# Where a minus sign is applied and who adds two small sums in the set-up of a state-space layer

## The chip, the cores and the metric

One core of a Trainium2 chip. The metric is device time in microseconds (us) for one launch of the whole program, as the median of several runs; lower is better. The engines are named as the profile names them: PE (TensorE matmul) and PEld (its weight loads), DVE (VectorE), ACT (ScalarE), POOL (GpSimd), SP (SyncE, which here only issues DMAs).

## What is computed

One encoder layer on 3 x 1024 tokens of width 1024: RMSNorm, one input projection, two parallel branches, an output projection, a residual and a final RMSNorm. Branch A is a gated MLP that mixes positions within chunks of 128. Branch B, which the change touches, is a diagonal complex state-space layer (S5): 64 groups of 16 channels, 64 complex states per group, one scan forward and one backward, a skip term D and a GELU.

```python
bb_re = fr[..., None] * b_re - fi[..., None] * b_im      # the input matrices B
bb_im = fr[..., None] * b_im + fi[..., None] * b_re
# scan: s[t] = a * s[t-1] + B x[t]     (complex, per state)
y = einsum('ntgp,gcp->ntgc', sr, c_re) - einsum('ntgp,gcp->ntgc', si, c_im)
y = (y_fwd + y_bwd) + d_skip * xb                        # D skip
```

Only the real part of C times the state is wanted, so the imaginary part of the state enters with a minus.

## The kernel before

**Blocks of 8 steps.** The S5 scan is done over blocks of 8 positions. For each group the kernel builds, once, an input matrix (8 x 16 inputs to the states), an output matrix with a real and an imaginary half (states to 8 x 16 outputs, powers of a times C), and a small kernel of 16 x 16 matrices for what happens within one block, whose diagonal matrix of lag 0 also carries D. They go to DRAM (`mat_d`, `ks_d`) and are read back in the second stage.

**First stage** (`p1`, up to about 372 us in the profiled execution). The main work on PE is the projection to the S5 input: 48 blocks of 24 matmuls of 128x512 (`sweep`, `mm3`, lines 59 to 61). Beside it run the norm of the token halves (`norm_half`, lines 253 to 292) and, one piece per matmul block, the generator `s5_setup`. Its first pieces make the powers and B and C; its last 32 pieces are the loop at lines 1026 to 1032: `build(gp)` makes the matrices for two groups, then `finish` completes those of the pair before.

**`build`** (lines 953 to 998). The real half `pc` number 0 is made by DVE: two products (967, 968) and their difference (970). The imaginary half, number 1, has its two products on POOL (967, 968), but its sum is made on DVE (972), as minus the first product minus the second, which puts the minus of the reference into the matrix. The products' buffers `m1`, `m2` of each half are single, so POOL's next products (989, 990, for the input matrix `pb`) wait until line 972 has read them. Line 991 adds them, on DVE for half 0 and on POOL for half 1. Line 997 copies B into zero-padded tiles `Bm`, four copies of 64x32 on POOL. The DMAs at line 975 (four per step) are issued by ACT.

**`finish`** (lines 1000 to 1023). Eight matmuls (1007) multiply `Bm` with `pc` into one PSUM tile `s5b`, of which there is one buffer. Two ACT copies (1010, 1011) bring it to SBUF as `ksb`; DVE adds the lag-0 part of the other direction straight from PSUM (1012); two DVE instructions (1015), one per group, add the identity scaled by D. Then a DMA, four PE transposes of `pb` into `s5a` (1020), an ACT copy and a DMA.

**Second stage.** `s5_groups` runs 64 groups beside the other projections; `states` (1107 to 1137) rotates, scans and rotates back the states: products at 1131 and 1132, then a difference for the real half (1133) and a sum for the imaginary half (1134).

A planner orders each engine's instructions when the program is built, by priority and the order of the code; at run time each engine works through its own list in that order and waits on semaphores. POOL also makes the low halves of the split weights (`whl`, line 152), which every matmul block needs.

Of the kernel before, what the change touches and what calls it, by code (L numbers as in the profile page):

```python
# [11 lines left out]
F32 = mybir.dt.float32  # L12
# [4 lines left out]
ALU = mybir.AluOpType  # L17
# [11 lines left out]
CH = 16  # L29
# [10 lines left out]
def bcast(ap, shape):  # L40
    return ap.to_broadcast(shape)
# [15 lines left out]
def mm3(nc, out, lh, ll, rh, rl, first, last):  # L57

    nc.tensor.matmul(out, lh, rh, start=first, stop=False)  # L59
    nc.tensor.matmul(out, lh, rl, start=False, stop=False)  # L60
    nc.tensor.matmul(out, ll, rh, start=False, stop=last)  # L61
# [699 lines left out]
def s5_setup(st, tc, a, xpool, ps, ident, kio, f8h, f8l, r8, ks_d, mat_d):  # L761
# [3 lines left out]
    V, S, G, T = nc.vector, nc.scalar, nc.gpsimd, nc.tensor  # L765
# [8 lines left out]
    dcol = mpool.tile([CH, GRP], F32, name="dcol")  # L774

    with ExitStack() as tmp_st:
# [7 lines left out]
        def tt(x, y, op, out=None):  # L784
            o = out if out is not None else new(x.shape)
            V.tensor_tensor(o, x, y, op=op)
            return o
# [82 lines left out]
        m2 = tt(mag, mag, ALU.mult)  # L870
# [44 lines left out]
        for t, n in ((Cr, "c_re"), (Ci, "c_im")):  # L915
            for q in range(2):
                craws = []
                for i in range(4):
                    raw = tp.tile([P, 2, 64], F32, name="craw", tag="craw", bufs=4)
                    g0 = 8 * (4 * q + i)  # L920
# [26 lines left out]
    wp = st.enter_context(tc.tile_pool(name="wp", bufs=2))  # L947
# [5 lines left out]
    def build(gp):  # L953
        g0 = 2 * gp
        gs = slice(g0, g0 + 2)

        sh = [P, 2, 9, CH]
        cr = bcast(Cr[:, gs].unsqueeze(2), sh)
        ci = bcast(Ci[:, gs].unsqueeze(2), sh)
        ar, ai = (bcast(t[:, :, gs].rearrange("p n g -> p g n").unsqueeze(3), sh) for t in AO)  # L960
        pcl = []
        for i, (u, v) in enumerate(((ar, ai), (ai, ar))):
            e = V if i == 0 else G
            m1 = wp.tile(sh, F32, tag=f"m1{i}", name="m1", bufs=1)
            m2 = wp.tile(sh, F32, tag=f"m2{i}", name="m2", bufs=1)
            pc = wp.tile(sh, F32, tag=f"pc{i}", name="pc")
            e.tensor_tensor(m1, cr, u, op=ALU.mult)
            e.tensor_tensor(m2, ci, v, op=ALU.mult)
            if i == 0:
                V.tensor_tensor(pc, m1, m2, op=ALU.subtract)  # L970
            else:
                V.scalar_tensor_tensor(pc, m1, -1.0, m2, op0=ALU.mult, op1=ALU.subtract)
            for d in range(2):
                r = slice(64 * d, 64 * d + 64)
                dma(mat_d[gs, r, 256 + P * i:384 + P * i].rearrange("g p (j c) -> p g (j c)", j=J),
                    pc[r, :, 1 - d:9 - d].rearrange("p g j c -> p g (j c)"))
            pcl.append(pc)

        sh = [P, 2, J, CH]
        br = bcast(Br[:, gs].unsqueeze(2), sh)  # L980
        bi = bcast(Bi[:, gs].unsqueeze(2), sh)
        ar, ai = (bcast(t[:, :, gs].rearrange("p n g -> p g n").unsqueeze(3), sh) for t in AI)
        pbs = []
        for i, (u, v) in enumerate(((ar, ai), (ai, ar))):
            m1 = wp.tile(sh, F32, tag=f"m1{i}", name="m1", bufs=1)
            m2 = wp.tile(sh, F32, tag=f"m2{i}", name="m2", bufs=1)
            pb = wp.tile(sh, F32, tag=f"pb{i}", name="pb")
            e = V if i == 0 else G
            e.tensor_tensor(m1, br, u, op=ALU.mult)
            e.tensor_tensor(m2, bi, v, op=ALU.mult)  # L990
            e.tensor_tensor(pb, m1, m2, op=ALU.subtract if i == 0 else ALU.add)
            pbs.append(pb)
        bm = Bm[gp % 2]
        for i, bt in enumerate((Br, Bi)):
            for d in range(2):
                r = slice(64 * d, 64 * d + 64)
                G.tensor_copy(bm[r, i, :, 32 * d:32 * d + 16], bt[r, gs])
        return gp, pcl, pbs, bm

    def finish(gp, pcl, pbs, bm):  # L1000
        g0 = 2 * gp
        gs = slice(g0, g0 + 2)

        pk = ps.tile([48, 2, 144], F32, tag="s5b", name="s5b")
        for g in range(2):
            for i in range(2):
                T.matmul(pk[:, g], bm[:, i, g], pcl[i][:, g].rearrange("p j c -> p (j c)"),
                         start=i == 0, stop=i == 1)
        ksb = wp.tile([CH, 2, 240], F32, tag="ksb", name="ksb", bufs=1)
        S.copy(ksb[:, :, 0:128], pk[32:48, :, 16:144])  # L1010
        S.copy(ksb[:, :, 128:240], pk[0:16, :, 16:128])
        V.tensor_tensor(ksb[:, :, 112:128], ksb[:, :, 112:128], pk[0:16, :, 0:16], op=ALU.add)
        for g in range(2):
            o = ksb[:, g, 112:128]
            V.scalar_tensor_tensor(o, ident[0:CH, 0:CH], dcol[:, g0 + g:g0 + g + 1], o, op0=ALU.mult, op1=ALU.add)
        dma(ks_d[gs].rearrange("g c o -> c g o"), ksb)
        pp = ps.tile([P, 2, 2, P], F32, tag="s5a", name="s5a")
        for i in range(2):
            for g in range(2):
                T.transpose(pp[:, g, i], pbs[i][:, g].rearrange("p j c -> p (j c)"), ident)  # L1020
        pbt = wp.tile([P, 2, 256], F32, tag="pbt", name="pbt", bufs=1)
        S.copy(pbt.rearrange("p g x -> p (g x)"), pp.rearrange("p g i x -> p (g i x)"))
        dma(mat_d[gs, :, 0:256].rearrange("g p x -> p g x"), pbt)

    last = None
    for gp in range(GRP // 2):
        cur = build(gp)
        if last:
            finish(*last)
        last = cur  # L1030
        yield
    finish(*last)


def s5_groups(tc, sp, ps, small, kio, f8h, f8l, r8, xb_d, ks_d, mat_d, gy_d):
# [3 lines left out]
    V, S, G, T = nc.vector, nc.scalar, nc.gpsimd, nc.tensor  # L1039
# [5 lines left out]
    gp = sp.tile([P, 2 * KK + 2], F32, name="gt")  # L1045
# [61 lines left out]
    def states(g):  # L1107
        u, mi = st[g]
        tb = st.pop(("tab", g))
        cs = tb[:, 0:1].to_broadcast(sh)  # L1110
        sn = tb[:, 1:2].to_broadcast(sh)

        pb = ps.tile([P, 2, 512], F32, tag="pb", name="pb")[:, :, 0:KK]
        for i in range(2):
            mm3(nc, pb[:, i], mi[:, 0, i], mi[:, 1, i], u[:, 0], u[:, 1], True, True)
        b1 = sp.tile(sh, F32, tag="b1", name="b1")
        b2 = sp.tile(sh, F32, tag="b2", name="b2")
        V.tensor_tensor(b1, pb, cs, op=ALU.mult)  # L1118
        V.tensor_tensor(b2, pb[:, ::-1], sn, op=ALU.mult)
        V.tensor_tensor(b1[:, 0], b1[:, 0], b2[:, 0], op=ALU.add)  # L1120
        V.tensor_tensor(b1[:, 1], b1[:, 1], b2[:, 1], op=ALU.subtract)
        dec = st.pop(("dec", g))
        bf = b1.rearrange("p i k -> p (i k)")
        for r, o, z in ((slice(0, 64), gp[:, 2:2 * KK + 2], (0, P)), (slice(64, 128), gp[:, 0:2 * KK], (P - 1, KK - 1))):
            f = slice(None, None, 1 if r.start == 0 else -1)
            V.tensor_tensor_scan(o[r, f], dec[r, f], bf[r, f], 0.0, op0=ALU.mult, op1=ALU.add)  # L1126
            V.memset(gt[r, :, z[0]:z[1] + 1:z[1] - z[0]], 0.0)
        h = sp.tile([P, 2] + sh[1:], F32R, tag="h", name="h", bufs=2)
        h1 = sp.tile(sh, F32, tag="b1", name="h1")
        h2 = sp.tile(sh, F32, tag="b2", name="h2")  # L1130
        V.tensor_tensor(h1, gt, cs, op=ALU.mult)  # L1131
        V.tensor_tensor(h2, gt[:, ::-1], sn, op=ALU.mult)  # L1132
        V.tensor_tensor(h1[:, 0], h1[:, 0], h2[:, 0], op=ALU.subtract)
        V.tensor_tensor(h1[:, 1], h1[:, 1], h2[:, 1], op=ALU.add)
        V.tensor_copy(h[:, 0], h1)
        V.tensor_tensor(h[:, 1], h1, h[:, 0].bitcast(F32), op=ALU.subtract)
        st[g] = u, h
# [33 lines left out]
    for g in range(GRP):  # L1171
        states(g)
        store()
        if g < GRP - 1:
            prepare(g + 1)
        if g % 2 == 0 and g < GRP - 2:
            tables(g + 2)
        if g % 2 == 1 and g < GRP - 1:
            finish_tables(g + 1)
        yield  # L1180
        if g:
            outputs(g - 1)
        if g < GRP - 1:
            prepare_out(g + 1)
            decay(g + 1)
        if g < GRP - 2:
            issue(g + 2)
        if g == GRP - 1:
            store()
            outputs(g)  # L1190
            store()
        yield
# [30 lines left out]
```

## Time and profile before

| | us |
|---|---|
| median of 3 runs | 2521.51 (2518.17 to 2525.8) |
| the profiled execution | 2519.67 |
| its span, first to last instruction | 2517.7 |
| PE busy | 2439.0 (97%) |
| DVE busy | 1771.5 (70%) |
| ACT busy | 974.3 (39%) |
| POOL busy | 638.2 (25%) |
| granted TensorE clock, mean | 0.990 of full |

How to read it: a busy share is a mean over stages with different limits. POOL is busy for a quarter of the whole, but nearly all of its work lies in the first stage. What a change to the first stage is worth is therefore read from windows of that stage, from the waits within it, and from the order of a few instructions.

### The profile page before, as it was taken

How to read it: one execution, taken by the hardware profiler on the slowest of the kernel's cores; microseconds unless marked ns; L12 is line 12 of the kernel's file. 1: busy time of each engine (PE TensorE's matmuls, PEld its weight loads, DVE VectorE, ACT ScalarE, POOL GpSimd, SP SyncE). 2: the span in 40 equal slices, each digit the busy share in tenths (PEclk: the TensorE clock that was granted, in tenths of full speed). 3: DMA queues.
4: the chain of work that ended last, by engine and by line, in shares of the span. 5: the costliest groups of instructions: out<-in, count | busy, mean ns of one | idle time of the engine just before them, and what ended most of it. 6: DMA issues, size and time to landing. Idle time of an engine off the chain costs nothing.

```text
span 2517.7 us, 34046 instructions
## 1 busy us (share of the span) xinstructions
PE 2439.0 (97%) x12313; PEld 2077.4 (83%) x12313; DVE 1771.5 (70%) x2921; ACT 974.3 (39%) x1738; POOL 638.2 (25%) x623
## 2 busy tenths in 40 slices
PE   7999999989999899999999999999999999999998
PEld 5777779978888798888899888887888888888886
DVE  6888856899999879988898989755555533333332
ACT  5343334544554534544454443424343411111110
POOL 2579873345334302311130321101000100000000
PEclk9999999999999999999999999999999999999999
DMA  9565455355555534444453444456465732222220
GB/s 243 178 187 145 143 162 183 118 173 176 184 169 198 170 110 129 143 160 144 139 171 119 127 136 149 135 168 181 134 184 158 234 109 93 92 96 94 96 76 30
DMA packets 363017, 367.21 MB, mean 146 GB/s; under 512 B 40768, under 2 KB 308576, under 8 KB 350560
## 3 DMA queue, kind: packets, MB, share of 16 engines
q1 hardware_dynamic: 311008, 343.99, 43.1%
q10 hardware_dynamic: 51840, 21.04, 3.5%
q8 instruction: 97, 1.59, 0.3%
q14 instruction: 72, 0.59, 0.1%
HBM read 229.76 MB, written 135.20 MB: 145 GB/s over the span
## 4 chain that ended last, share of the span: by engine, by line
PE 70%; DVE 15%; DMA 2%; issue 1%; POOL 1%; ACT 1%; SPq 0%; ACTq 0%; DVEq 0%; POOLq 0%
PE mm L59 18%; PE mm L61 18%; PE mm L60 18%; PE acc L59 3%; PE acc L60 3%; PE acc L61 3%; DVE gt L1126 3%; PE py L59 1%; PE py L61 1%; PE py L60 1%; DVE h L1132 1%; DVE v L578 1%; DVE h L1131 1%; DVE b L1118 1%; DVE v L479 1%
## 5 line engine op out<-in xcount | busy, mean ns | idle before, releaser
L59 PE MATMUL mm<-w,yh 128*128 128x512 f32 x768 | 302.6, 394 | 0.0
L60 PE MATMUL mm<-w,yh 128*128 128x512 f32 x768 | 301.8, 393 | 0.0
L61 PE MATMUL mm<-w,yh 128*128 128x512 f32 x768 | 301.3, 392 | 0.0
L59 PE MATMUL mm<-ha,whl 128*128 128x512 f32 x704 | 278.3, 396 | 8.4 <-DVE v L503 7.4
L59 PE MATMUL mm<-hb,whl 128*128 128x512 f32 x704 | 278.0, 395 | 6.0 <-DVE v L503 6.0
L61 PE MATMUL mm<-ha,whl 128*128 128x512 f32 x704 | 275.9, 392 | 1.3 <-POOL whl L152 1.3
L60 PE MATMUL mm<-ha,whl 128*128 128x512 f32 x704 | 275.9, 392 | 0.0
L60 PE MATMUL mm<-hb,whl 128*128 128x512 f32 x704 | 275.8, 392 | 0.0
L61 PE MATMUL mm<-hb,whl 128*128 128x512 f32 x704 | 275.6, 392 | 0.0
L1126 DVE TENSOR_TENSOR_SCAN gt<-dec,b 64x768 f32<-64x768 f32 x128 | 232.2, 1814 | 3.1
L152 POOL TENSOR_TENSOR whl<-wf,whl 128x512 fp32r<-128x512 f32 x112 | 171.9, 1549 | 231.4 <-ACT whl L151 198.5
L61 PEld LDWEIGHTS mm<-w,yh 128*128 128x128 f32 x768 | 144.3, 188 | 33.7
L59 PEld LDWEIGHTS mm<-w,yh 128*128 128x128 f32 x768 | 144.1, 188 | 33.2
L60 PEld LDWEIGHTS mm<-w,yh 128*128 128x128 f32 x768 | 144.2, 188 | 33.0
L700 DVE SCALAR_TENSOR_TENSOR yh<-yf,yh 128x512 fp32r<-128x512 f32 x96 | 66.8, 699 | 147.6 <-ACT yh L699 106.0
L1057 POOL TENSOR_TENSOR mo<-m,mo 128x384 fp32r<-128x384 f32 x64 | 86.5, 1351 | 321.2 <-ACT mo L1056 321.2
L729 DVE TENSOR_TENSOR xr<-xr,mm 128x512 f32<-128x512 f32 x48 | 33.0, 688 | 184.1 <-PE mm L61 184.1
L59 PEld LDWEIGHTS mm<-ha,whl 128*128 128x128 f32 x704 | 133.1, 189 | 35.3 <-DVE v L503 8.3
L59 PEld LDWEIGHTS mm<-hb,whl 128*128 128x128 f32 x704 | 133.3, 189 | 32.1 <-DVE v L503 7.0
L61 PEld LDWEIGHTS mm<-ha,whl 128*128 128x128 f32 x704 | 133.0, 189 | 29.6 <-POOL whl L152 1.7
L61 PEld LDWEIGHTS mm<-hb,whl 128*128 128x128 f32 x704 | 133.2, 189 | 28.0
L60 PEld LDWEIGHTS mm<-ha,whl 128*128 128x128 f32 x704 | 133.2, 189 | 26.6 <-DVE ha L288 0.9
(243 smaller groups left out, 5946.1 us busy)
## 6 DMA issues: line engine op xcount, KB each, us to landing
whl<-wc_d SPq DMA_DIRECT2D x64, 1024.0 KB
wc_d<-whl SPq DMA_DIRECT2D x32, 1024.0 KB
wf<-in_w_in_dram SPq DMA_DIRECT2D x112, 256.0 KB
m<-mat_d SPq DMA_DIRECT2D x128, 128.0 KB
xb_d<-xo SPq DMA_DIRECT2D x24, 512.0 KB
U<-xb_d SPq DMA_DIRECT2D x64, 192.0 KB
gy_d<-gy SPq DMA_DIRECT2D x64, 192.0 KB
zb_d<-zb SPq DMA_DIRECT2D x24, 512.0 KB
```

Source lines behind the costliest of these rows:

```text
L59: nc.tensor.matmul(out, lh, rh, start=first, stop=False)
L60: nc.tensor.matmul(out, lh, rl, start=False, stop=False)
L61: nc.tensor.matmul(out, ll, rh, start=False, stop=last)
L152: G.tensor_tensor(flat[:, 1, sl], wf, flat[:, 0, sl].bitcast(F32), op=ALU.subtract)
L479: V.tensor_scalar(v, v, rs[:, q:q + 1], nb[:, q:q + 1], op0=ALU.mult, op1=ALU.add)
L578: V.scalar_tensor_tensor(t, t, LG[:, fb:fb + 1], RB[:, fb:fb + 1].to_broadcast([P, 4, P]), op0=ALU.mult, op1=ALU.add)
L700: V.scalar_tensor_tensor(y[:, 1], yf, sc, y[:, 0].bitcast(F32), op0=ALU.mult, op1=ALU.subtract)
L729: V.tensor_tensor(x, x, t.ps[i], op=ALU.add)
L1057: eng.tensor_tensor(t[:, 1], src, t[:, 0].bitcast(F32), op=ALU.subtract)
L1118: V.tensor_tensor(b1, pb, cs, op=ALU.mult)
L1126: V.tensor_tensor_scan(o[r, f], dec[r, f], bf[r, f], 0.0, op0=ALU.mult, op1=ALU.add)
L1131: V.tensor_tensor(h1, gt, cs, op=ALU.mult)
```

## The change

The minus of the imaginary output half is taken out of the matrix and put into the two things it is multiplied with. The sum at line 972 becomes a plain sum on the engine that made its products, POOL. The imaginary B is written into `Bm` times -1 (POOL, `tensor_scalar` for `tensor_copy`), and in the second stage the imaginary state is written as minus the one term minus the other (DVE, `scalar_tensor_tensor` for `tensor_tensor`). Apart from that, POOL makes in `build` a tile `dg` of 16 x 2 x 16 with D on the diagonals, and `finish` adds it to the PSUM part (`l0`) and that to `ksb`: two DVE additions in place of one addition and two scaled ones.

```diff
             e.tensor_tensor(m1, cr, u, op=ALU.mult)
             e.tensor_tensor(m2, ci, v, op=ALU.mult)
-            if i == 0:
-                V.tensor_tensor(pc, m1, m2, op=ALU.subtract)
-            else:
-                V.scalar_tensor_tensor(pc, m1, -1.0, m2, op0=ALU.mult, op1=ALU.subtract)
+            e.tensor_tensor(pc, m1, m2, op=ALU.subtract if i == 0 else ALU.add)
...
-                G.tensor_copy(bm[r, i, :, 32 * d:32 * d + 16], bt[r, gs])
-        return gp, pcl, pbs, bm
-
-    def finish(gp, pcl, pbs, bm):
+                if i == 0:
+                    G.tensor_copy(bm[r, i, :, 32 * d:32 * d + 16], bt[r, gs])
+                else:
+                    G.tensor_scalar(bm[r, i, :, 32 * d:32 * d + 16], bt[r, gs], -1.0, None, op0=ALU.mult)
+
+        dg = wp.tile([CH, 2, CH], F32, tag="dg", name="dg")
+        G.tensor_tensor(dg, ident[0:CH, 0:CH].unsqueeze(1).to_broadcast([CH, 2, CH]),
+                        dcol[:, gs].unsqueeze(2).to_broadcast([CH, 2, CH]), op=ALU.mult)
+        return gp, pcl, pbs, bm, dg
+
+    def finish(gp, pcl, pbs, bm, dg):
...
-        V.tensor_tensor(ksb[:, :, 112:128], ksb[:, :, 112:128], pk[0:16, :, 0:16], op=ALU.add)
-        for g in range(2):
-            o = ksb[:, g, 112:128]
-            V.scalar_tensor_tensor(o, ident[0:CH, 0:CH], dcol[:, g0 + g:g0 + g + 1], o, op0=ALU.mult, op1=ALU.add)
+        l0 = wp.tile([CH, 2, CH], F32, tag="l0", name="l0", bufs=1)
+        V.tensor_tensor(l0, dg, pk[0:16, :, 0:16], op=ALU.add)
+        V.tensor_tensor(ksb[:, :, 112:128], ksb[:, :, 112:128], l0, op=ALU.add)
...
-        V.tensor_tensor(h1[:, 1], h1[:, 1], h2[:, 1], op=ALU.add)
+        V.scalar_tensor_tensor(h1[:, 1], h1[:, 1], -1.0, h2[:, 1], op0=ALU.mult, op1=ALU.subtract)
```

## Rows read from the trace of the kernel before

**Rows 1.** Busy time by stretch: us, then each engine's (x count), PEclk, DMA share, GB/s.
```profile
core 0: us, PE busy (x) PEld busy (x) DVE busy (x) ACT busy (x) POOL busy (x), PEclk, DMA share, GB/s
94.00:207.00 113.00, 103.27 (x510) 82.12 (x508) 96.75 (x195) 44.48 (x90) 92.32 (x130) 0.95 0.62 187
...
303.00:358.00 55.00, 53.54 (x272) 42.38 (x271) 35.76 (x78) 16.61 (x36) 51.43 (x74) 1.00 0.55 155
...
600.00:1640.00 1040.00, 1022.12 (x5522) 906.04 (x5521) 925.63 (x1293) 485.53 (x837) 259.01 (x191) 0.99 0.47 150
```

**Rows 2.** PE's waits, 90 to 372 us: total us, times, longest us.
```profile
PE s5b L1007 <- DVE ksb L1012: 7.8, 7, 1.4
PE tr L283 <- DVE x L275: 4.0, 5, 2.3
PE s5b L1007 <- DVE rxa L51: 2.6, 1, 2.6
```

**Rows 3.** PE's instructions in order: start us, duration us, [idle before it, releaser].
```profile
319.70 0.54 PE L1007 MATMUL s5b<-pc,Bm 128*48 128x144 f32 x3 [1.44 <-DVE ksb L1012]
...
341.28 1.15 PE L1007 MATMUL s5b<-pc,Bm 128*48 128x144 f32 x8
342.36 0.66 PE L1020 MATMUL s5a<-ident,pb 128*128 128x128 f32 x4
```

**Rows 4.** DVE's instructions in order, ahead of the wait at 319.70.
```profile
317.23 1.53 DVE L972 SCALAR_TENSOR_TENSOR pc<-m,m 128x288 f32<-128x288 f32 x1 [3.42 <-POOL m L968]
318.69 0.42 DVE L989 TENSOR_TENSOR m<-Br,AI 128x256 f32<-128x256 f32 x1
...
319.38 0.17 DVE L1012 TENSOR_TENSOR ksb<-ksb,s5b 16x32 f32<-16x32 f32 x1
```

**Rows 5.** POOL's instructions in order, two stretches.
```profile
317.16 1.29 POOL L152 TENSOR_TENSOR whl<-wf,whl 128x512 fp32r<-128x512 f32 x1
...
338.02 0.73 POOL L991 TENSOR_TENSOR pb<-m,m 128x256 f32<-128x256 f32 x1
338.83 0.71 POOL L967 TENSOR_TENSOR m<-Cr,AO 128x288 f32<-128x288 f32 x1
339.49 0.71 POOL L968 TENSOR_TENSOR m<-Ci,AO 128x288 f32<-128x288 f32 x1
```

**Rows 6.** POOL's waits, 90 to 372 us: total us, times, longest us.
```profile
POOL m L989 <- DVE pc L972: 16.4, 8, 6.0
...
POOL whl L152 <- ACT whl L151: 6.4, 4, 3.3
POOL m L989 <- DVE rxy L53: 2.1, 1, 2.1
```

**Rows 7.** Groups of POOL, then of DVE, 90 to 372 us: busy us, mean ns | idle before.
```profile
L997 POOL COPY Bm<-Bi 64x32 f32<-64x32 f32 x64 | 26.7, 417 | 3.2
L968 POOL TENSOR_TENSOR m<-Ci,AO 128x288 f32<-128x288 f32 x32 | 26.2, 818 | 0.0
...
L972 DVE SCALAR_TENSOR_TENSOR pc<-m,m 128x288 f32<-128x288 f32 x32 | 25.3, 790 | 28.1 <-POOL m L968 20.5 <-DMA mat_d<-pc 3.4 <-DMA x<-in_x_sample_dram 2.1
```

**Rows 8.** Single lines of the whole execution: duration ns min/median/max, first and last start.
```profile
L972 DVE SCALAR_TENSOR_TENSOR pc<-m,m x32: 439/459/1551, 99.3 to 354.6; 128x288 f32<-128x288 f32 x32
...
L970 DVE TENSOR_TENSOR pc<-m,m x32: 439/760/1374, 97.8 to 349.8; 128x288 f32<-128x288 f32 x32
...
L1012 DVE TENSOR_TENSOR ksb<-ksb,s5b x32: 167/169/177, 117.6 to 366.8; 16x32 f32<-16x32 f32 x32
...
L1015 DVE SCALAR_TENSOR_TENSOR ksb<-ident,dcol,ksb x64: 215/217/699, 118.1 to 367.1; 16x16 f32<-16x16 f32 x64
...
L997 POOL COPY Bm<-Br x64: 202/329/675, 98.4 to 354.8; 64x32 f32<-64x32 f32 x64
```

**Rows 9.** DVE's instructions in order, second stage.
```profile
665.28 0.55 DVE L1134 TENSOR_TENSOR h<-h,h 128x384 f32<-128x384 f32 x1
665.75 0.60 DVE L1067 SCALAR_TENSOR_TENSOR tab<-kio,f8h,tab 128x384 f32<-128x384 f32 x1
```

## The prediction

> **What bounds the kernel now.** I read the busy time by stretch first [rows 1]. PE is busy over 97% of the span, so any gain must come out of PE's gaps. The stretch where nearly all of the changed code runs, 94 to 358 us, is different from the rest: POOL, a quarter busy over the whole, is at 92.3 of 113 us at its beginning and at 51.4 of 55 at its end, while DVE falls from 96.8 of 113 to 35.8 of 55. The reader is to see that the engine which gets work is the fuller one, the one which gives it the emptier one, at least late in the stage.
>
> Second, what PE waits for there [rows 2]: 7.8 us in seven waits of the product s5b for the DVE addition at line 1012 (s5b has one buffer, so the next product waits until line 1012 has read it), 4.0 us for normalised rows, 2.6 us for a DVE chain of the norm. That is what this change can win on PE directly.
>
> Third, why line 1012 is late [rows 3 to 5]. At 317.16 POOL starts a weight split of 1.29 us. At 317.23 DVE starts line 972, for whose products it had been idle 3.42 us; it needs 0.44 us when it runs alone [rows 8] but takes 1.53, until 0.3 us after POOL's split has ended at 318.45. Lines 989 and 990 follow, then line 1012 at 319.38, and PE starts at 319.70, 0.15 us after its end and after 1.44 us of waiting. DVE is not slow: it waits for POOL's products, then for POOL's split.
>
> **What holds two engines apart.** Line 1012, with one operand in PSUM, takes 167 to 177 ns all 32 times; line 1015, with both tensors in SBUF, 215 to 699; the two sums at lines 970 and 972 from 439 up to 1374 and 1551 [rows 8]. POOL's products go from about 0.66 us (one start to the next at 338.83 and 339.49 [rows 5]) to a mean of 0.82 [rows 7]. DVE instructions with two SBUF inputs and POOL's take turns.
> The Trainium skill (SBUF — State Buffer, "Who interferes with whom") says so: a DVE instruction with two SBUF inputs contends with a GpSimd instruction that reads SBUF, and whichever starts second is blocked for the whole of the other. The rows agree (1.53 us against 0.44). It speaks against the change as well as for it, since the sum moved to POOL occupies the shared read longer than it did on DVE.
>
> **Part by part.**
> *Sum of the imaginary half to POOL, 32 times.* DVE loses 25.3 us (32 x 0.79) and the 28.1 us of idle time ahead of it [rows 7], none of which counts by itself, as DVE is not PE's limit but through line 1012. POOL gets a 128x288 sum: at least 0.66 us (the product's spacing), 0.82 (its mean) at most; since it reads what was just written, as line 991 does (0.73 us and 0.81 to the next start for 256 columns), I take 0.80: 25.6 us. Behind it on POOL stand the weight splits and the next products.
> *dg on POOL, 32 times, 16x32.* No row shows it. The nearest is the copy of 64x32: 0.20 us at best, 0.42 in the mean where it reads the imaginary B [rows 7, 8]; above stands a full two-operand instruction of 0.66. I take 0.30, near the copy: 9.6 us (6.4 to 21). Its two buffers make POOL wait for l0 of two steps before; Bm has the same wait already, for the product that l0 reads, so I cost it at nothing; if DVE is late it would cost up to the 1.4 us of one such wait.
> *-1 in two of the four Bm copies.* Same shape and input: 0 to 0.1 us each, taken 0.05: 3.2 us.
> *D and lag 0.* DVE loses 2 x 0.215 us per step and keeps two small additions; the read of s5b no longer stands behind the ACT copies. POOL is relieved by what the two engines contend for.
> *Second stage, 64 times.* A scaled sum with a constant costs what a plain one does (439 ns for both at lines 970 and 972). Against it, line 1067 takes 0.60 us beside 0.55 for line 1134 [rows 9], but its factor is read from a tile. So 0, at most 64 x 0.05 = 3.2 us on a DVE that is busy 925.6 of 1040 us there [rows 1].
>
> **The sum on POOL.** Added: 25.6 + 9.6 + 3.2 = 38 us (27 to 54). Given back: the 16.4 us in which POOL waited for line 972 to release the products [rows 6], all of it, because sum and products now follow each other on one engine. Given back by contention: a step has some 11 POOL instructions, stretched by about 0.16 us each (0.82 less 0.66), 1.8 us, or 56 us over 32 steps; DVE's two-input work in a step is four instructions of 0.44 us, three of 0.42 and two of 0.215, 3.45 us, of which 0.44 + 0.43 less one new addition of 0.17 goes, a fifth: 11 us. The ends are 0 and 32 x 0.87 = 28. POOL's waits for ACT's casts and for the norm (6.4 + 2.1 [rows 6]) shrink when POOL runs later; I take half, 4 us. Net: 38 - 16 - 11 - 4 = 7 us later at the end of the set-up.
> **What PE sees of it.** POOL's line 991 of one step ends at 338.75 and the transposes that need it start at 342.36 [rows 3, 5], so 3.6 us of lag are hidden. That leaves +3 us if POOL sets the end of the stage. Before that end PE is freed of the 7.8 us, so that it arrives at POOL's limit instead of DVE's. Where POOL had waits to lose (up to 6.0 us in one [rows 6]) PE gains; where POOL was full (303 to 358 us [rows 1]) PE loses again. The two estimates, +3 by the ledger and -8 by PE's waits, bracket the answer; the larger of the two rules at each point, and POOL's ledger is the more uncertain. I forecast no measurable change, -1 us on the profiled 2519.67, which stands 1.8 us under the median of 2521.51: **2521 us** as the median.
>
> **The rivals.**
> *A, faster.* POOL keeps ahead because contention gives back 20 us or more, and PE is free: the 7.8 us go, the 2.6 us behind the norm chain and half of the 4.0 too, since DVE has some 34 us less to do (25.3 + 64 x 0.217 less 32 x 0.17): -12 us, 2509. For it: DVE no longer waits for POOL at all. Against it: POOL at 51.4 of 55 us.
> *B, slower: POOL becomes the limit of the first stage.* If contention gives back nothing and the small instructions cost 0.4 to 0.5 us, POOL's added 1.4 us a step make 45 us; less 16.4, 4 and 3.6 that is +21 us, 2542; with half of the 11 us, +15: 2537. It decides from the point where added work less relief passes 24 us in 32 steps, 0.75 us a step. For it: late in the stage nothing but those 3.6 us stands between POOL and PE. Against it: the means from which its prices come already hold contention that partly goes.
> *C, the state's sign costs.* 64 x 0.05 on DVE would be +3 us; inside the range of the forecast.
> *D, it does nothing.* The seven waits at line 1012 stay, because l0 still stands behind other DVE work, and POOL's work is hidden: within 3 us of 2521.
>
> **How the numbers follow.** About 0.3%, 7.6 us, is what a measurement can tell from no change. The forecast with C and D: 0.50, its own range 2514 to 2529. A: 0.25, reaching from 2513 down to 2506. B: 0.25, from 2530 to 2542. The range takes in most of A and the lower half of B: 2510 to 2535. Faster 0.25, the same 0.50, slower 0.25.
>
> **What would show it.** Right: line 972 stands on POOL at 0.7 to 0.85 us; POOL's wait for it (16.4 us) is gone, and PE's seven waits for line 1012 too; DVE's busy time over 94 to 358 us falls by some 34 us while POOL's rises by 20 to 30; line 1134 stays at 0.55. Wrong: new PE waits at s5b or s5a that name POOL (rival B), waits at s5b that still name DVE (D), dg or the negated copies above 0.6 us, or a difference that lies after 400 us, where I expect none.

## The result and the profile after

| | before | after |
|---|---|---|
| median, us | 2521.51 | 2538.38 (2535.8 to 2542.6) |
| the profiled execution | 2519.67 | 2542.6 |
| its span | 2517.7 | 2540.3 |
| POOL busy | 638.2 | 668.8 |
| DVE busy | 1771.5 | 1784.8 |
| granted TensorE clock, mean | 0.990 | 0.988 |

The ratio is 1.0069, with a 95% interval of 1.0058 to 1.0079: some 17 us slower, where no measurable change was forecast and the range ended at 2535. The time lies between the two that rival B worked out (2537 and 2542). The profiled execution after is the slowest of its five, so the profiles differ by more than the medians, by 22.6 us of span.

First, busy time by stretch, after, to be laid beside [rows 1]; the second fence is one line of before, over the stretch up to its last s5b product, and the last line of the first fence is its counterpart.

```profile
core 0: us, PE busy (x) PEld busy (x) DVE busy (x) ACT busy (x) POOL busy (x), PEclk, DMA share, GB/s
94.00:207.00 113.00, 95.83 (x454) 75.86 (x453) 93.27 (x160) 40.81 (x83) 100.45 (x146) 0.92 0.59 176
...
303.00:358.00 55.00, 48.05 (x235) 37.61 (x233) 42.14 (x61) 17.03 (x37) 51.48 (x81) 0.97 0.48 132
600.00:1640.00 1040.00, 1017.87 (x5501) 901.86 (x5500) 931.97 (x1297) 488.52 (x842) 261.92 (x194) 0.99 0.47 151
94.00:383.60 289.60, 258.58 (x1273) 205.67 (x1271) 221.62 (x365) 102.69 (x212) 259.65 (x386) 0.96 0.54 155
```

```profile
94.00:362.76 268.76, 252.01 (x1275) 201.72 (x1273) 211.47 (x429) 102.96 (x212) 230.15 (x322) 0.98 0.56 164
```

The last s5b product of the set-up starts at 383.60 instead of 362.76: 20.8 of those 22.6 us lie before it. Up to there PE runs the same work (1273 and 1275 instructions recorded). Its idle time grew from 16.75 us (268.76 - 252.01) to 31.02, +14.3; its busy time from 252.0 to 258.6, +6.6, at a granted clock of 0.96 in place of 0.98. Two thirds of the loss are waits and one third is slower matmuls.

PE's waits, 90 to 390 us (total us, times, longest us), to be laid beside [rows 2]:

```profile
PE s5b L1011 <- DVE l L1017: 19.5, 8, 6.1
PE s5b L1011 <- DVE rxa L51: 3.4, 1, 3.4
...
PE tr L283 <- DVE x L275: 1.6, 3, 0.8
PE s5b L1011 <- POOL Bm L997: 1.3, 2, 0.9
```

The 7.8 us behind line 1012 did not go. They became 19.5 us behind its successor, line 1017, the longest 6.1 in place of 1.4. And a wait costs PE more than itself. PE's instructions in order around the longest one, and the busy time by stretch there (columns as above):

```profile
123.16 2.12 PE L1011 MATMUL s5b<-pc,Bm 128*48 128x144 f32 x8 [6.05 <-DVE l L1017]
...
126.55 0.63 PE L60 MATMUL mm<-hx,whl 128*128 128x512 f32 x1
...
129.41 0.39 PE L59 MATMUL mm<-hx,whl 128*128 128x512 f32 x1
```

```profile
117.00:124.00 7.00, 0.94 (x5) 0.76 (x5) 6.82 (x18) 0.10 (x1) 4.92 (x8) 0.85 0.98 325
124.00:131.00 7.00, 7.00 (x26) 5.47 (x25) 3.55 (x8) 4.72 (x9) 5.75 (x10) 0.66 0.44 119
126.50:127.50 1.00, 1.00 (x4) 0.75 (x3) 0.00 (x0) 0.83 (x2) 0.84 (x4) 0.50 0.99 357
129.00:131.00 2.00, 2.00 (x10) 1.64 (x9) 1.36 (x3) 1.35 (x3) 2.00 (x3) 1.00 0.10 22
```

PE was busy 0.94 of 7 us; in the next 7 us, without a gap, the granted clock is 0.66 in the mean and PE gets 26 instructions through. The 128x512 product takes 0.63 us at 126.55, at the lower of the clock's two levels (granted 0.50, 1.2 GHz), and 0.39 at 129.41, at the upper one (granted 1.00, 2.4 GHz).

POOL's groups, 90 to 390 us (busy us, mean ns | idle before), and below them single lines of the whole execution (ns min/median/max, first and last start), for [rows 7] and [rows 8]:

```profile
L969 POOL TENSOR_TENSOR pc<-m,m 128x288 f32<-128x288 f32 x32 | 30.2, 944 | 1.9
L997 POOL TENSOR_SCALAR Bm<-Bi 64x32 f32<-64x32 f32 x64 | 28.3, 442 | 3.3
L968 POOL TENSOR_TENSOR m<-Ci,AO 128x288 f32<-128x288 f32 x32 | 25.8, 806 | 0.0
L995 POOL COPY Bm<-Br 64x32 f32<-64x32 f32 x64 | 22.5, 351 | 6.3 <-PE s5b L1011 4.4
L1000 POOL TENSOR_TENSOR dg<-ident,dcol 16x32 f32<-16x32 f32 x32 | 13.0, 406 | 2.3 <-DVE l L1017 2.2
```

```profile
L969 POOL TENSOR_TENSOR pc<-m,m x32: 778/864/1382, 100.1 to 374.0; 128x288 f32<-128x288 f32 x32
L1000 POOL TENSOR_TENSOR dg<-ident,dcol x32: 228/415/913, 100.9 to 377.5; 16x32 f32<-16x32 f32 x32
L1137 DVE SCALAR_TENSOR_TENSOR h<-h,h x64: 541/550/1656, 423.0 to 1681.7; 128x384 f32<-128x384 f32 x64
```

The sum takes 0.94 us in the mean, dg 0.41; the 16.4 us of [rows 6] are gone; the products of line 968 take 806 ns as against 818 [rows 7]; other instructions of POOL became shorter by more, as the account below shows. In the second stage the scaled state sum has a median of 550 ns, as the single row of line 1134 in [rows 9] led to expect.

### The profile page after: what moved, and what is told of

Its sections match the earlier page's. It is cut to its first block, busy times and chain, and to the rows that moved or that the text cites. A ratio compares the mean times of both kernels' runs of the same rounds, so it can differ in the third digit from the quotient of the medians.

```text
span 2540.3 us, 34052 instructions
## 1 busy us (share of the span) xinstructions
PE 2448.3 (96%) x12313; PEld 2083.3 (82%) x12313; DVE 1784.8 (70%) x2857; ACT 974.1 (38%) x1738; POOL 668.8 (26%) x687
## 4 chain that ended last, share of the span: by engine, by line
PE 70%; DVE 14%; DMA 2%; issue 1%; POOL 1%; ACT 0%; SPq 0%; DVEq 0%; ACTq 0%; POOLq 0%
PE mm L59 19%; PE mm L61 18%; PE mm L60 18%; PE acc L59 3%; PE acc L60 3%; PE acc L61 3%; DVE gt L1129 3%; PE py L59 1%; PE py L60 1%; PE py L61 1%; DVE h L1135 1%; DMA whl<-wc_d 1%; DVE v L578 1%; DVE v L479 1%; DVE h L1134 1%
## 5 line engine op out<-in xcount | busy, mean ns | idle before, releaser
L59 PEld LDWEIGHTS mm<-ha,whl 128*128 128x128 f32 x704 | 132.6, 188 | 35.4 <-DVE v L503 9.5
L59 PEld LDWEIGHTS mm<-hb,whl 128*128 128x128 f32 x704 | 133.5, 190 | 33.1 <-DVE v L503 7.0
L61 PEld LDWEIGHTS mm<-ha,whl 128*128 128x128 f32 x704 | 132.6, 188 | 29.6 <-POOL whl L152 1.7
L61 PEld LDWEIGHTS mm<-hb,whl 128*128 128x128 f32 x704 | 133.3, 189 | 28.1
L60 PEld LDWEIGHTS mm<-hb,whl 128*128 128x128 f32 x704 | 133.7, 190 | 27.1 <-DVE hb L288 1.8
```

## The experiments

Four theories stand in the expectations. **1**: what POOL has more to do sets the pace of the set-up. **2**: DVE's two-input instructions are shut out while POOL runs several of its own in a row. **3**: the new addition l0 waits for POOL's dg. **4**: the sum comes late for ACT, which stands in its list before the DMAs that store it, with the copies of ksb behind them, for which DVE and then PE wait. An engine's list is its instructions in their order. PE's and SP's are the same in all these kernels, save for the two DMA issues a step that one kernel moves to SP and for tile names; what the planner redraws are the lists of DVE, POOL and ACT. The partner of a kernel is the one that its edit starts from. Differences to before below are the ratio less one, times 2521 us.

**One part at a time.** The state's and B's sign alone, with a plain sum at line 972 on DVE:

```diff
-                V.scalar_tensor_tensor(pc, m1, -1.0, m2, op0=ALU.mult, op1=ALU.subtract)
+            V.tensor_tensor(pc, m1, m2, op=ALU.subtract if i == 0 else ALU.add)
```

> Only the sign is moved (B negated by POOL, state negated by DVE); the second sum stays on DVE as a plain sum, D is added as before. If the sign itself costs nothing (the prediction): 2519 to 2525 us. If the negated copies or the negated state cost: 2526 or more, with line 1134 above 0.55 us or the Bi copies well above 0.42 us.

2522.52 us, 1.0002 (0.9993 to 1.0012). The sign is free, on POOL and in the second stage.

The same with the sum on POOL:

```diff
+            e.tensor_tensor(pc, m1, m2, op=ALU.subtract if i == 0 else ALU.add)
```

> The sign and the sum on POOL, D as before. Theory 1 (POOL's added load in the set-up, of which the sum is the larger part, sets PE's pace): most of the 17 us is here, 2531 to 2538 us. Theory 2 (a run of two-input POOL instructions without a break shuts DVE out for 2.7 to 6.0 us at a time, because line 972 no longer breaks the run): the whole of it, 2535 to 2540 us, with single DVE instructions of over 2.5 us in the set-up. Theory 3 (the wait of l0 for POOL's dg): little of it, 2518 to 2526 us.

2539.23 us, 1.0069 (1.0053 to 1.0086): the whole loss. It is the loss of the sum with the order that the planner drew for it: 67 of DVE's other instructions and 14 of POOL's stand elsewhere than in the kernel with the sign alone. Only dg and l0 on the kernel before:

```diff
+        G.tensor_tensor(dg, ident[0:CH, 0:CH].unsqueeze(1).to_broadcast([CH, 2, CH]),
...
+        V.tensor_tensor(l0, dg, pk[0:16, :, 0:16], op=ALU.add)
+        V.tensor_tensor(ksb[:, :, 112:128], ksb[:, :, 112:128], l0, op=ALU.add)
```

> Only D's diagonal made by POOL and added with l0; the second sum stays on DVE with its minus. Theory 1: dg's 0.41 us a step on a full POOL, 2522 to 2530 us. Theory 2: no DVE instruction over 2 us, 2516 to 2524 us. Theory 3: most of the 17 us, 2532 to 2540 us, with PE waiting for l0 and l0 for POOL.

2523.36 us, 1.0010 (1.0001 to 1.0019). The changed kernel with dg made by DVE:

```diff
-        G.tensor_tensor(dg, ident[0:CH, 0:CH].unsqueeze(1).to_broadcast([CH, 2, CH]),
+        V.tensor_tensor(dg, ident[0:CH, 0:CH].unsqueeze(1).to_broadcast([CH, 2, CH]),
```

> The changed kernel with dg made by DVE instead of POOL, so that l0 waits for no POOL instruction. Theory 1: POOL has 13 us less to do, 2530 to 2536 us. Theory 2: the shut-outs stay, 2534 to 2540 us. Theory 3: 2518 to 2526 us.

2535.43 us, 1.0057 (1.0042 to 1.0072). Theory 3 falls as the main cause: D costs some 2 to 3 us. Theory 2 falls with the kernel with sign and sum on POOL, in which no DVE instruction of the set-up takes over 1.8 us and which is as slow as the whole change.

**How the sum gets to PE.** Waits of the kernel with sign and sum on POOL, 90 to 390 us, PE's and DVE's; then the instructions of ACT, POOL, DVE and PE in order at one of them:

```profile
PE s5b L1007 <- DVE ksb L1012: 19.0, 10, 4.5
...
DVE ksb L1012 <- ACT ksb L1011: 35.1, 10, 8.0
```

```profile
360.74 4.09 ACTq L972 DMA_DIRECT2D mat_d<-pc  x3
...
361.74 0.93 POOL L995 COPY Bm<-Br 64x32 f32<-64x32 f32 x2
...
362.75 0.80 POOL L969 TENSOR_TENSOR pc<-m,m 128x288 f32<-128x288 f32 x1
...
364.87 0.62 ACT L151 CAST whl<-wf 128x512 fp32r<-128x512 f32 x1 [6.49 <-POOL Bm L997]
...
366.89 0.34 ACT L1011 COPY ksb<-s5b 16x224 f32<-16x224 f32 x1
...
367.26 0.18 DVE L1012 TENSOR_TENSOR ksb<-ksb,s5b 16x32 f32<-16x32 f32 x1 [4.66 <-ACT ksb L1011]
...
367.58 1.15 PE L1007 MATMUL s5b<-pc,Bm 128*48 128x144 f32 x8 [1.57 <-DVE ksb L1012]
```

ACT reaches the stores at 360.74, but POOL makes the sum only from 362.75 to 363.55, behind its copies; casts and copies follow, ksb is there at 367.23, DVE has waited 4.66 us and PE 1.57. Here the sum's lateness reaches PE through the lists of POOL, ACT and DVE. In before the sum ahead of these stores was DVE's.

Two kernels took the stores of the imaginary half out of ACT's way by issuing them a step later, in `finish`, with a third buffer, in the changed kernel and in the kernel before:

```diff
-                dma(mat_d[gs, r, 256 + P * i:384 + P * i].rearrange("g p (j c) -> p g (j c)", j=J),
...
+            if i == 0:
+                store_pc(gs, i, pc)
...
+        store_pc(gs, 1, pcl[1])
```

> The changed kernel, but the two DMAs that store the second out matrix are issued by ACT one step later, in finish, where POOL's sum is long done (three buffers for it). Theory 4 (route: POOL is late, ACT's queue waits in these DMA issues for POOL's sum, and the copies of s5b behind them, line 1012's successor and so PE are late): 2518 to 2527 us, with DVE's waits for ACT's copy of ksb well under the 35 us that the sum alone on POOL shows. Theory 1 (POOL's load itself sets the pace, by any route): 2532 to 2540 us.

> The kernel before, with the two DMAs of the second out matrix issued one step later by ACT, as in e5_defer. If ACT's queue waiting for the second matrix is part of the 7.8 us for which PE waits at s5b in the kernel before: 2512 to 2518 us. If not: 2519 to 2524 us.

2553.92 us, 1.0121 (1.0100 to 1.0143), and 2538.91 us, 1.0068 (1.0052 to 1.0084). Both are slower than their partners, the other way than theory 4 had it. The lists of POOL and ACT, and in the second DVE's, were redrawn, and in the second, without any sum on POOL, ACT again waited in the stores for DVE's part, so they say nothing of theory 4 by themselves. The second shows something else: no engine has work added there, and the moved stores with the order that came of them (some 60 instructions each of DVE and POOL elsewhere) cost 17 us, as much as the whole change. So a redrawn order is a rival for part of the loss. No run has the sum on POOL with DVE's list as it is without it, so its share is not separated.

The changed kernel with POOL's other sum, line 988, given to DVE in exchange:

```diff
-            e.tensor_tensor(pb, m1, m2, op=ALU.subtract if i == 0 else ALU.add)
+            V.tensor_tensor(pb, m1, m2, op=ALU.subtract if i == 0 else ALU.add)
```

> The changed kernel, but the second sum of the input matrices (line 988, 128x256) is made by DVE, so that POOL's load is about that of before plus dg: POOL gets one sum and gives one. Theory 1: 2520 to 2528 us. Theory 4: the DMA issues still wait for POOL's sum, 2530 to 2538 us.

2539.93 us, 1.0072 (1.0055 to 1.0090). POOL's load falls, but DVE now waits 35.3 us for POOL's products there, and nothing is won, where theory 1 expected 2520 to 2528.

**Load alone.** The kernel before with one unused sum of 128x288 a step on POOL, with an unused memset of 128x576 on POOL, and with the unused sum on DVE:

```diff
+        G.tensor_tensor(spare, Cr[:, gs].unsqueeze(2).to_broadcast([P, 2, 9, CH]),
+                        Ci[:, gs].unsqueeze(2).to_broadcast([P, 2, 9, CH]), op=ALU.add)
```
```diff
+        G.memset(spare, 0.0)
```
```diff
+        V.tensor_tensor(spare, Cr[:, gs].unsqueeze(2).to_broadcast([P, 2, 9, CH]),
+                        Ci[:, gs].unsqueeze(2).to_broadcast([P, 2, 9, CH]), op=ALU.add)
```

> The kernel before with one more POOL instruction per step, a sum of 128x288 whose result nobody uses, behind POOL's last sum of the step (32 more in all). The work of the kernel is otherwise that of before, the second out matrix is summed on DVE. Theory 1: POOL's load alone makes it slow, 2530 to 2538 us. Theory 4: only the place of the sum on the way to ACT's DMA issue counts, 2519 to 2527 us.

> The kernel before with one unused POOL memset of 128x576 per step (32 in all; nothing reads it), which reads no SBUF. By the memsets seen before (206 ns for 128 elements, 99 for one) it should take about 0.5 to 0.6 us, 16 to 20 us in all. Theory 1 in its plain form (time in POOL's queue): +12 to +20 us, 2534 to 2542. Rival (what costs is the SBUF read that POOL and DVE take turns at, not the time in the queue): 0 to +5 us, 2521 to 2527.

> The kernel before with one unused sum of 128x288 per step on DVE (32 in all; its result is read by nothing), the counterpart of the same load on POOL, which cost 27.7 us for 30.3 us of work. Theory 1 (POOL's queue paces the set-up, DVE has room): DVE is busy about 211 of 264 us in 94 to 358 us, so 15 to 30 us more of DVE work costs at most a third of itself, 0 to 8 us: 2521 to 2530. Rival (any extra instruction with two SBUF inputs slows both engines, or any redrawn order costs this much): +15 to +28 us, 2537 to 2550.

In the first two, every engine has the list of before, plus 32 instructions on POOL; in the third DVE's has 21 of its instructions elsewhere and ACT's two. The sum on POOL (32 x 946 ns, 30.3 us): 2549.17 us, 1.0108 (1.0092 to 1.0124), +27 us, more than the 2530 to 2538 that theory 1 expected. The memset (32 x 588 ns, 18.8 us): 2529.18 us, 1.0034 (1.0021 to 1.0047), +9 us. The sum on DVE: 2532.91 us, 1.0049 (1.0032 to 1.0067), +12 us. At unchanged lists POOL's time costs, 0.9 us for each us of a two-input sum and 0.5 for the memset, which reads nothing. The memset lies between its two expectations; DVE's 12 us are over the 0 to 8 of theory 1, so DVE has no free room either, but the same sum costs less than half there. A stretch of the first of them shows POOL full, with PE and DVE busy for little more than a third and ACT hardly at all; the second line is the same stretch of before (columns as above):

```profile
120.00:150.00 30.00, 10.98 (x36) 8.00 (x36) 11.67 (x26) 2.12 (x5) 28.19 (x39) 0.66 0.24 66
120.00:150.00 30.00, 26.32 (x129) 20.61 (x129) 22.64 (x51) 12.41 (x26) 21.94 (x34) 0.94 0.57 175
```

**The sum's duration alone.** Two kernels with the sign and the sum on POOL, in which the imaginary half lies in two tiles cleared at the start; in the second the sum covers only 160 of 288 columns:

```diff
-            w = pc if i == 0 else pc
-            e.tensor_tensor(w, m1 if i == 0 else m1, m2 if i == 0 else m2, op=ALU.subtract if i == 0 else ALU.add)
+            w = pc if i == 0 else pc[:, :, 0:5]
+            e.tensor_tensor(w, m1 if i == 0 else m1[:, :, 0:5], m2 if i == 0 else m2[:, :, 0:5], op=ALU.subtract if i == 0 else ALU.add)
```

> The sign moved and the sum on POOL, D as before, with the imaginary half in two tiles that are allocated once and cleared at the start instead of two rotating buffers. Theory 1 (time on POOL) and the rival (the order drawn by the planner) both expect about what the sign and the sum together gave: 2532 to 2543 us. It is the partner of the next kernel.

> The partner with the sum on POOL over 160 of 288 columns (blocks 0 to 4 of 9; the other columns of the imaginary half keep the zeros of the start, so that part of its output is left out). Every engine has the same instructions in the same order as in the partner; only line 973 is shorter, 0.55 to 0.6 us in place of 0.94, about 11 to 12 us in 32 steps. Theory 1 (the duration on POOL sets the pace): 7 to 12 us under the partner. Rival (what costs is the order, or where DVE, ACT and PE wait in it, whatever the sum takes): within 3 us of the partner.

2539.56 us, 1.0079 (1.0064 to 1.0094), and 2531.21 us, 1.0046 (1.0031 to 1.0061). Every engine has the same list; line 973 differs in its width, and two of its 32 instances stand one place away from where they were on POOL. Groups of the sum on POOL, 90 to 400 us, first and second kernel:

```profile
L973 POOL TENSOR_TENSOR pi<-m,m 128x288 f32<-128x288 f32 x32 | 31.8, 995 | 1.9
```

```profile
L973 POOL TENSOR_TENSOR pi<-m,m 128x160 f32<-128x160 f32 x32 | 23.7, 740 | 1.9
```

8.1 us less on POOL (less than the 11 to 12 expected, as a column costs only 2 ns) make the run 8.4 us shorter. With the unused sum this is the cleanest evidence for theory 1: at unchanged lists more time on POOL costs, and a shorter sum there saves.

**Taking other work off POOL.** B's copies to DVE, in the kernel before and in the changed one:

```diff
-                G.tensor_copy(bm[r, i, :, 32 * d:32 * d + 16], bt[r, gs])
+                V.tensor_copy(bm[r, i, :, 32 * d:32 * d + 16], bt[r, gs])
```

> The kernel before with the four copies of B into the padded tiles (line 997) made by DVE in place of POOL: 26.7 us less on POOL, some 128 x 0.1 to 0.2 = 13 to 25 us more on DVE. Theory 1: the load on POOL falls, so the set-up comes earlier, as far as PE leaves room: PE waits 7.8 us for line 1012 in the first stage; -3 to -10 us, 2511 to 2518. Rival (before was not limited by POOL, only what is added counts): 0 to +3 us, 2521 to 2525, or slower if the copies arrive late because DVE has them behind its own sums.

> The changed kernel with the four copies into the padded tiles on DVE (copies for the real, times -1 for the imaginary part): POOL gives back the 28.3 + 26 us of lines 995 and 997, about as much as the change put on it (30.6 us net). Theory 1: nearly all of the 16.9 us goes: 2519 to 2526. Rival (the sum on POOL hurts by where it stands, between the products and the DMA issue on ACT, whatever POOL's total): 2532 to 2540.

2538.34 us, 1.0070 (1.0055 to 1.0085), and 2545.93 us, 1.0098 (1.0083 to 1.0114): both slower than their partners, against theory 1's expectation. In the first, POOL is down to 168.14 of 264 us (94 to 358), DVE is at 244.87, and POOL waits 58.6 us for line 972: DVE has become the limit, with the lists of before but for these copies and two instructions.

Two copies of 64x64 in place of four of 64x32, in the kernel before, in the changed one (B's imaginary part negated once at the start) and in the one with sign and sum alone:

```diff
-                G.tensor_copy(bm[r, i, :, 32 * d:32 * d + 16], bt[r, gs])
+            G.tensor_copy(bm[r, :, :, 32 * d:32 * d + 16], Bri[r, :, gs])
```

> The kernel before with B's two parts in one tile, so that two copies of 64x64 a step take the place of four of 64x32 on POOL. By the least time of a copy (202 ns) and its mean (0.34 to 0.42 us) it takes 0.2 to 0.3 us each off POOL, 13 to 20 us in all, and puts nothing on DVE. Theory 1: the gain shows as far as PE waited for the set-up: -3 to -8 us, 2513 to 2518. Rival (the kernel before is balanced so that POOL's load decides only upward, or the order decides): 2518 to 2524.

> The changed kernel with B's imaginary part negated once at the start (one DVE instruction of 128x1024, the two sums of the input matrix turned round to match) and both parts in one tile, so that two plain copies of 64x64 a step take the place of two copies and two products with -1 of 64x32: some 28 us less on POOL in 32 steps, nothing more on DVE in the steps. Theory 1 (the loss is POOL's load, about one to one while POOL is the fuller engine): nearly all of the 17 us comes back, 2519 to 2526. Rival (the loss belongs to the route of the sum, between the products and the DMA issue on ACT): at most a third comes back, 2532 to 2538.

> The same two copies with the sign and the sum on POOL alone, D as before. POOL's load is then 13 us under that of the kernel above. Theory 1: 2517 to 2524, at or under the kernel before. Rival (the route of the sum): 2531 to 2538.

2522.87 us, 1.0008 (0.9999 to 1.0018); 2539.43 us, 1.0073 (1.0059 to 1.0087); 2532.09 us, 1.0042 (1.0030 to 1.0055). POOL gave up 25 to 26 us of copies in each, and the kernels got back nothing, nothing and some 7 us, where theory 1 expected 2513 to 2518, 2519 to 2526 and 2517 to 2524. From the first kernel POOL's waits, from the third the stretch up to its last s5b product:

```profile
POOL m L989 <- DVE pc L972: 29.9, 11, 6.9
POOL whl L152 <- ACT whl L151: 23.5, 9, 10.0
```

```profile
94.00:375.89 281.89, 259.38 (x1273) 204.60 (x1271) 214.94 (x397) 103.78 (x214) 230.47 (x290) 0.96 0.54 158
```

In the kernel before, the time won is waited away: POOL's wait for line 972 grows from 16.4 us [rows 6] to 29.9. In the other two it goes into waits for ACT's casts: up to the last s5b product, without the first wait at 94 us, 18.2 us against 6.3 in the partner, and 27.1 against 11.8. And in the third kernel POOL is as busy as in before (230.47 and 230.15 us) and still 11 us are lost. So POOL's total is not the measure: theory 1 holds for the sum and for what is added, not for any us of POOL. This is not the work of a new order: the lists are those of the partners, but for the copies and, in the second and third kernel, for the one negation and for three DVE and two ACT instructions before 94 us.

**Without the link through ACT.** Sign and sum on POOL, the stores of the imaginary half issued by SP:

```diff
-                dma(mat_d[gs, r, 256 + P * i:384 + P * i].rearrange("g p (j c) -> p g (j c)", j=J),
+                (dma if i == 0 else nc.sync.dma_start)(mat_d[gs, r, 256 + P * i:384 + P * i].rearrange("g p (j c) -> p g (j c)", j=J),
```

> The sign and the sum on POOL, D as before, but the two DMAs that store the imaginary half are issued by SP instead of ACT, so that ACT no longer stands waiting for POOL's sum with the copies of ksb behind it. The order on PE is that of the kernel with the sign and the sum, on DVE and POOL nearly so. Theory 4 (the sum costs by holding ACT's list): DVE's waits for the ksb copies (35.1 us in ten) fall under 15 us, PE's waits at s5b (19.0) under 10, and the time by 8 to 18 us, 2521 to 2531. Rival (POOL's own queue, whose sum delays the weight splits and the next products directly): the waits move to POOL's instructions and the time stays within 4 us of 2539; or SP now waits for the sum and its loads of weights and tokens come late, 2540 to 2550.

2530.55 us, 1.0033 (1.0021 to 1.0045): half of the loss is back. DVE's list has 16 instructions elsewhere, POOL's four. Its waits as above, and the stretch up to the last s5b product:

```profile
PE s5b L1007 <- DVE ksb L1012: 15.9, 12, 5.0
...
DVE ksb L1012 <- ACT ksb L1011: 34.2, 9, 8.2
```

```profile
94.00:374.23 280.23, 254.46 (x1276) 202.62 (x1276) 221.73 (x397) 103.78 (x213) 256.27 (x354) 0.98 0.54 157
```

The time is within theory 4's range, the waits are not: those for ksb hardly fall (35.1 to 34.2) and those at s5b go to 15.9, not under 10. PE's idle time is 25.8 us against 29.4 (289.09 less 259.66) in its partner, and its busy time 254.5 against 259.7, since the clock stays at 0.98. That the way through ACT carries part of the loss is likely by the time alone; the waits that were to prove it do not, so theory 4 stays half open.

## Why the prediction was wrong, point by point

**What bounds it.** Right as to the stage: the difference lies before 384 us. That nearly all of POOL's work lies in the first stage, as stands ahead of the prediction, is not so: 249 of its 638 us lie before the last s5b product in before, and 259 between 600 and 1640 us [rows 1]. Nothing else hangs on it, since the sums go by stretches of the first stage.

**The ledger of POOL** came out 14 us too low: 7 us later at the end of the set-up, where the last s5b product is 20.8 us late. The step that failed is the 20 us of waits that it booked as given back (16.4 for line 972 and 4 for casts and norm); 8.7 came back. POOL's busy time up to the last s5b product rose by 29.5 us, against 38 - 11 = 27 in the ledger, near it by two errors of opposite sign. Groups of POOL before, 94 to 362.76 us, then after, 94 to 383.60 us, so each with the 34 weight splits and the 32 steps up to that product:

```profile
L152 POOL TENSOR_TENSOR whl<-wf,whl 128x512 fp32r<-128x512 f32 x34 | 49.5, 1470 | 20.9 <-DMA hs_d<-hf 12.6 <-ACT whl L151 6.4 <-DMA mat_d<-pc 1.4
L989 POOL TENSOR_TENSOR m<-Br,AI 128x256 f32<-128x256 f32 x32 | 30.6, 955 | 20.0 <-DVE pc L972 16.4 <-DVE rxy L53 2.1
L990 POOL TENSOR_TENSOR m<-Bi,AI 128x256 f32<-128x256 f32 x32 | 29.3, 916 | 0.0
```

```profile
L152 POOL TENSOR_TENSOR whl<-wf,whl 128x512 fp32r<-128x512 f32 x34 | 45.8, 1359 | 18.6 <-DMA hs_d<-hf 12.2 <-ACT whl L151 6.3
L986 POOL TENSOR_TENSOR m<-Br,AI 128x256 f32<-128x256 f32 x32 | 25.6, 799 | 2.1
L987 POOL TENSOR_TENSOR m<-Bi,AI 128x256 f32<-128x256 f32 x32 | 25.3, 792 | 0.0
```

- *Added work, 38 us.* Measured 45.5: 30.2 for the sum, 13.0 for dg and 2.3 for the negation (28.3 + 22.5 against 26.7 + 21.8 in before). The sum was taken at 0.80 us and takes 0.94, above every row that served as a bound; dg was taken at 0.30 "near the copy" and takes 0.41, the copy's mean and not its minimum.
- *Given back by contention, 11 us.* It came, and was a little more: POOL's four products a step fell from 111.3 to 101.2 us, nearly all of it in the two behind the sum (59.9 to 50.9 in the fences), and the weight splits from 49.5 to 45.8; its other sum stayed (25.8 and 26.1). That is 13.5 us (45.5 less 13.5 is 32 by the rows; the records of neighbouring instructions overlap a little, so busy time rose by 29.5). Those two products take 46.7 to 51.5 us in each of the eleven kernels with the sum on POOL and 51.8 to 59.9 in each of the nine with it on DVE. The working was not as good as its result: it took a step as 11 instructions of POOL, where 322 in 32 steps are 10, and it counted on less two-input work on DVE, and DVE's instructions were held longer (line 988 takes 922 ns in the mean there, 538 as line 991 in before; the new addition at line 1018 takes 421 ns, not 170).
- *Given back by waits, 16.4 and 4 us.* The wait for line 972 is gone, and the norm's 2.1; the casts' is 6.3 us for 6.4. But POOL's idle time in these stretches fell only from 38.6 to 29.9 us. New waits came, 4.4 us for PE ahead of Bm and 2.2 for DVE ahead of dg (in the groups above). The prediction saw the wait ahead of dg and cost it at nothing, because Bm had such a wait already; that the one ahead of Bm would grow it did not see.
- Together +29.5 busy and -8.7 idle are the 20.8 us. That must come out so, since busy and idle time fill the stretch, and it is no proof that POOL sets the pace: taking copies off POOL gave much less than such a ledger would.

**What PE sees.** The forecast set POOL's +3 beside PE's -8 and let them meet near nought. The second step that failed is the -8: the waits behind line 1012 were read as the price of DVE's sum, to vanish with it. They are where lateness of ACT's copies and of POOL arrives too (19.0 us in the kernel with sign and sum, behind the same old line 1012), and they grew to 19.5 us. The text also lets the larger of the two rules decide at each point, which would have been the +3, and then forecasts -1. Of the 3.6 us of lag that were to hide POOL's lateness nothing shows: the last s5b product is 20.8 us late and the span 22.6 us longer. Also missing: PE's slower matmuls after its waits, 6.6 of the 20.8 us.

**Rival A** fell: nothing of the 7.8 us came free, and DVE's busy time over 94 to 358 us went from 210.5 to 209.3, not down by 34. Up to the last s5b product it even rose, from 211.5 to 221.6 us, with 64 instructions fewer. **C** and the -1 at Bm: right, the sign is free (1.0002). **D's part** by itself: right that it costs little, 2.5 us. **Rival B** was right in place and in its price of the added work (1.4 us a step). That its +15 to +21 us fit is partly luck: at +21 it let contention give back nothing, where 13.5 us came back, and it too took the 20 us of waits as gone. What spoke against it ("the means already hold contention that partly goes") came true. Its mechanism, POOL as the limit, is borne out for work that is added to POOL, and not for work that is taken off.

**What was to show it.** Of the signs of a right forecast, POOL's wait gone and the second stage unchanged came true. The sum at 0.94 us lies above the 0.7 to 0.85, and over 94 to 358 us POOL's busy time rose by 11.1 us (227.2 to 238.3), not by 20 to 30; that window now ends before the set-up does. Of the signs of a wrong one, waits at s5b that name POOL (rival B) came with 1.3 us in two. Those that name DVE came with 19.5 us, and were listed as the mark of rival D, "it does nothing"; they marked a loss, through DVE's place at the end of the chain.

## What to carry to other kernels

Price work that is given to the fuller engine by the mean of its longest likely row: here the price was 7.5 us short. Do not book an engine's waits as given back because the cause they name goes: of 20 us on POOL 8.7 came back, and PE's 7.8 us at the end of the chain became 19.5. A wait is no stock of time that goes with one of its causes; ask who is late next. When two engines are both near full, moving work either way costs (DVE to POOL +17 us, POOL to DVE +18 us here), and a neighbour's time is worth something only where it lies in the chain.

## What the runs showed of the hardware

DVE can be held through a whole run of POOL instructions. POOL's list and one DVE instruction, in order, changed kernel:

```profile
347.07 0.70 POOL L967 TENSOR_TENSOR m<-Cr,AO 128x288 f32<-128x288 f32 x1
...
352.22 0.63 POOL L987 TENSOR_TENSOR m<-Bi,AI 128x256 f32<-128x256 f32 x1
352.81 0.89 POOL L995 COPY Bm<-Br 64x32 f32<-64x32 f32 x2
```

```profile
347.12 6.03 DVE L988 TENSOR_TENSOR pb<-m,m 128x256 f32<-128x256 f32 x1
```

Line 988 takes 0.41 us at its shortest and 6.03 here: it starts 0.05 us after the first of seven two-input POOL instructions that follow each other without a gap, and ends at 353.15, in POOL's first copies into Bm. The Trainium skill (SBUF — State Buffer, "Who interferes with whom") has the second of the two engines blocked for the whole of the other's instruction; here it was seven instructions. What makes a hold so long is not shown: in the set-ups of all kernels, two-input DVE instructions of over 1.9 us stand in three alone, all with dg on POOL (longest 6.03, 6.23 and 2.99 us), and three others with dg on POOL have none. Such holds were not the cause of the loss: the kernel with sign and sum alone has none of them and is as slow.

A POOL sum of 128 columns fewer saved 255 ns (995 to 740), 2 ns a column; by that, as an estimate, some 0.42 us of the 128x288 sum do not depend on its width. A POOL sum of 16x32 takes 228 ns at least and 415 in the median: narrow tiles cost nearly as much as that.
